# The last norm of an encoder kernel: the last chunk's squares to TensorE in their own parts, a Newton step in two operations, additions split evenly, one program order

## The chip, the core and the metric

The kernel runs on one core of a Trainium2 chip. The metric is the device time of one execution in microseconds (us), lower is better. Three runs of the kernel before took 3162.19, 3160.36 and 3156.84 us; the median is 3160.36 us.

## The reference

One layer over a prompt of 2048 tokens and a sample of 32, 2080 columns in all, with 1024 channels. Attention and gated linear attention come first, then the channel sub-layer. Only the last lines of the layer matter here: a gated MLP gives `yf`, and its RMSNorm, gated per channel, is added to the residual.

```
def rmsnorm(x, g):
    xf = x.astype(jnp.float32)
    r = lax.rsqrt(jnp.mean(xf * xf, axis=-1, keepdims=True) + EPS)
    return (xf * r).astype(x.dtype) * g
...
    yf, conv_new = conv_ffn(h, s_conv, p['w_up'], p['w_dw'], p['b_dw'], p['w_down'])
    x = x + gate_f * rmsnorm(yf, p['g_post_ffn'])
```

## The kernel before, in words

Channels lie on the 128 partitions, tokens along the free dimension; the 1024 output channels are 8 chunks of 128. The tokens are worked in three passes (`p` = 0, 1, 2), and each pass holds two segments of up to 348 columns (`s` = 0, 1), the upper and the lower half of a `[128, 2, 348]` tile. Products are done in a Strassen-like scheme, each in float32r as three matmuls per 128 rows (a high part and a low part of each operand). `prod` (L1869) issues one such product; its matmuls are all recorded at L1882.

The program runs through `UNITS`: first the up projections of the three passes, then nine units of the down projection, each with four blocks `m`. One `block` (L1975) makes four quarter results at once: chunk `m` in `ad` (segment 0 in `ad[:, 0]`, segment 1 in `ad[:, 1]`) and chunk `m + 4` in `g`. In the down projection three units (groups 0 to 2) add up in `ACC[p, c]`, which lies in SBUF. `down_sum` (L1947) does that: VectorE adds the PSUM result to `ACC` (L1955), and in the last group ScalarE squares the sum into `sq` (L1970), VectorE adds the square to the running sum `sa` (L1972), and ScalarE multiplies `ACC` by the gate (L1968, in place). `sa` is thus a sum over chunks, still spread over 128 partitions.

The order is written out by hand. `put(n, f)` appends a step to a list, and `run_due()`, called in every `side()`, takes the steps that are due: with n = 0 at once, with n over 0 at the (n+1)th call. From L1224 on, a `manual_schedule` named `ordered` fixes this order as the program order of TensorE, ScalarE, VectorE, GpSimd and SyncE. It is closed at L2268, ahead of the last steps; from there on only TensorE keeps program order (L82), and the scheduler of the framework orders the instructions of the other engines. `in_order[0] = False` (L2269) makes every `put` immediate.

The last steps belong to the last block of the last unit (pass 2, `last` in the code). It makes chunk 3 in `ad` and chunk 7 in `g`. In order of time: segment 1 of chunk 7 is ready after product S3 (L2013), segment 0 of chunk 3 after product A12, segment 1 of chunk 3 after S4 and the addition L2019, segment 0 of chunk 7 after A22 (L2035). Then `finish(2)` (L2145) does the last norm:

- for each segment, segment 1 first: `split` (L67) makes a high part of `sa` on ScalarE (L69) and a low part on VectorE (L72); two matmuls with a matrix of ones sum both over the partitions into PSUM (L2154, L2155);
- for each segment: Ln and Exp on ScalarE give a first value `r0` of 1/sqrt (L2158, L2159), and three operations on VectorE make a Newton step of it in PSUM (L2160 to L2162);
- for each segment and each of the 8 chunks in `ORDER` = 0, 4, 1, 5, 2, 6, 3, 7: VectorE multiplies `ACC` by the result, from PSUM (L2166), the residual `xs` is added, both operands in SBUF (L2168; positions 2 and 5 on VectorE, the other six on GpSimd), and `move` (L2050) stores the segment with DMAs from the queues of SyncE and ScalarE (L2057). The two stores at the very end, of chunks 3 and 7 in segment 0, are on ScalarE's queue.

The residuals `xs` are loaded some 40 us before the end, and the activation table that holds Ln and Exp is preloaded at the same place (L2249, L2250).

Of the kernel before, what the change touches and what calls it, by code (L numbers as in the profile page):

```python
# [13 lines left out]
AF = mybir.ActivationFunctionType  # L14
OP = mybir.AluOpType
# [4 lines left out]
D = 1024  # L20
KD = 8
TP, TS = 2048, 32
# [5 lines left out]
EPS = 1e-6  # L28
# [15 lines left out]
def f32(ap):  # L44
    return ap.bitcast(F32)
# [13 lines left out]
def encoder_step(ctx: ExitStack, tc: tile.TileContext, I, O):  # L59
    nc = tc.nc  # L60
# [6 lines left out]
    def split(hi, lo, src, keep=False):  # L67

        i = nc.scalar.activation(hi, src, AF.Copy)  # L69
        if keep and not in_order[0]:  # L70
            tc.keep_in_program_order(i)
        nc.vector.tensor_sub(lo, src, f32(hi))  # L72
# [19 lines left out]
    ones = consts.tile([128, 128], F32R, name="ones")  # L92
# [150 lines left out]
    with ExitStack() as st:  # L243
# [115 lines left out]
        r0 = fin0()  # L359
# [1509 lines left out]
    def prod(out, u, m, x, y, first):  # L1869

        while (u, m, x) not in WO or (u, y) not in HO:
            if (u, m, x) not in WO:
                next(wq)
            else:
                hstep()
            run_due()
        wh, wl = WO[u, m, x]
        hi, lo = HO[u, y]
        w, n = WIDTH[u], NK[u]
        for k in range(n):  # L1880
            for i, (l_, r_) in enumerate(((wh, hi), (wh, lo), (wl, hi))):
                nc.tensor.matmul(out[:, :w], l_[:, k], r_[:, k, :w], start=first and k == 0 and i == 0,  # L1882
                                 stop=k == n - 1 and i == 2, skip_group_check=True)
        del LIVE[u, m, x]
        if m == NM[u] - 1:
            del HLIVE[(7 * u + OPS.index(y)) % len(HP)]
# [16 lines left out]
    def act_sums():  # L1903

        if made:
            p, j, x, y = made.pop(0)
            o = WP[p] - 2
            x0, x1, y0, y1 = x[:, 0, :o], x[:, 1, :o], y[:, 0, :o], y[:, 1, :o]

            for i, (out, a, b) in enumerate(((x0, x1, x0), (x1, y1, x1), (y1, y1, x0), (y0, y0, y1))):  # L1910
                put(i, lambda out=out, a=a, b=b: nc.vector.tensor_sub(out, a, b))
            for i, v in ((0, x), (2, y)):
                put(3 + i, lambda i=i, v=v: nc.sync.dma_start(
                    dap(aT, ((4 * p + i) * 11 + j) * 128 * SEG, [[SEG, 128], [11 * 128 * SEG, 2], [1, o]]), v[:, :, :o]))
# [11 lines left out]
    def up_g(p, m, x, y, before):  # L1926

        o, c, d = WP[p] - 2, m + MF, 1

        def act():  # L1930
            nc.vector.tensor_mul(y[:, :, :o], y[:, :, :o], YG[:, :, :o])
            soon(2, lambda: nc.sync.dma_start(actD[p, m, :, :, :o], y[:, :, :o]))
            if m % 2:
                made.append((p, m // 2, before, y))

        if p == 2:
            put(1, lambda: conv_outputs(x[:, 1], c))
        put(d + 1, lambda: tap(2, YG, x, c, o))
        put(d + 2, lambda: tap(1, YG, x, c, o))
        put(d + 3, lambda: tap(0, YG, x, c, o))  # L1940
        put(d + 4, act)
# [5 lines left out]
    def down_sum(p, grp, c, x, first, seg=None, n=0):  # L1947

        o = WP[p] - 2
        if grp == 0:  # L1950
            ACC[p, c] = spare.pop(0)
            put(n, lambda: nc.scalar.copy(ACC[p, c][:, :, :o], x[:, :, :o]))
            return
        a, x, q, t = [v[:, :, :o] if seg is None else v[:, seg, :o] for v in (ACC[p, c], x, sa if first else sq, sa)]
        put(n, lambda: nc.vector.tensor_add(a, a, x))  # L1955
        if grp == 2:
            flat = ACC[p, c].rearrange("p s w -> p (s w)")
            e = SEG + TP - segs[5][0]
            if p < 2:
                parts = [(0, a)]  # L1960
            elif seg is None:
                parts = [(0, flat[:, :e]), (1, flat[:, e:])]
            else:
                parts = [[(0, flat[:, :SEG])], [(0, flat[:, SEG:e]), (1, flat[:, e:])]][seg]

            def gate():
                for s, v in parts:
                    nc.scalar.activation(v, v, AF.Copy, scale=mod[:, 5, c, s:s + 1])  # L1968

            put(n + 1, lambda: nc.scalar.activation(q, a, AF.Square))  # L1970
            if not first:
                put(n + 2, lambda: nc.vector.tensor_add(t, t, q))  # L1972
            put(n + 2, gate)

    def block(u, m, prev, side):  # L1975

        p, grp = UNITS[u]
        at_step[0] = 0  # L1980
        w = WIDTH[u]
        last = u == len(UNITS) - 1 and m == NM[u] - 1
        ad = psA.tile([128, 2, 512], F32, name="ad", tag="ad")
        g = psG.tile([128, 2, 512], F32, name="g", tag="g")
        prod(ad[:, 0], u, m, "A11", "B11", True)
        norm = wanted.pop(0)(ad, g) if wanted else None
        if u == 0 and m < 2:

            nc.tensor.matmul(g[:, 0], WO[u, m, "A11"][0][:, 0], WO[u, m, "A11"][0].rearrange("p k n -> p (k n)"),
                             start=True, stop=True, skip_group_check=True)  # L1990
        nc.scalar.copy(g[:, 0, :w], ad[:, 0, :w])  # L1991
        if norm:
            norm()
        if prev:
            prev[0]()
        side()
        if prev:
            prev[1]()
        side()
        if not prev:  # L2000

            prod(ad[:, 1], u, m, "S1", "T1", True)
        prod(g[:, 0], u, m, "S2", "T2", False)
        nc.scalar.copy(U2[:, :w], g[:, 0, :w])  # L2004
        side()
        if prev:
            prod(ad[:, 1], u, m, "S1", "T1", True)
        nc.scalar.copy(P5[:, :w], ad[:, 1, :w])  # L2008
        side()
        prod(g[:, 0], u, m, "S3", "T3", False)  # L2010
        nc.vector.tensor_add(g[:, 1, :w], g[:, 0, :w], P5[:, :w])
        if last:
            down_sum(p, grp, m + 4, g, False, 1)  # L2013
        side()
        prod(ad[:, 0], u, m, "A12", "B21", False)
        act_sums()
        side()
        prod(ad[:, 1], u, m, "S4", "B22", False)
        nc.vector.tensor_add(ad[:, 1, :w], ad[:, 1, :w], U2[:, :w])  # L2019
        side()  # L2020
        if grp is None:
            YA.append(YA.pop(0))
            before, ya = YA[-2:]

        def rest_ad():
            if grp is None:
                up_ad(p, m, ad, ya)
            elif last:
                for seg in (1, 0):
                    down_sum(p, grp, m, ad, False, seg)  # L2030
            else:
                down_sum(p, grp, m, ad, m == 0, None, 0)

        def rest_g():
            prod(g[:, 0], u, m, "A22", "T4", False)  # L2035
            if grp is None:
                up_g(p, m, g, ya, before)
            else:
                down_sum(p, grp, m + 4, g, False, 0 if last else None, 1)

        return rest_ad, rest_g

# [26 lines left out]
    def post(p):  # L2069
# [55 lines left out]
        for i, m in enumerate(ORDER):  # L2125
# [16 lines left out]

            put(2, store)

    def finish(p):  # L2145

        o = WP[p] - 2
        sh, sl = [x[:, 0:2, :o] for x in HP[(7 * len(UNITS)) % len(HP)]]
        r0 = sq[:, :, :o]
        rs = {}  # L2150
        for s, ps, tag in ((1, psA, "ad"), (0, psG, "g")):
            split(sh[:, s], sl[:, s], sa[:, s, :o])
            rs[s] = q = ps.tile([128, 2, 512], F32, name=tag, tag=tag)[:, s, :o]
            nc.tensor.matmul(q, ones, sh[:, s], start=True, stop=False)  # L2154
            nc.tensor.matmul(q, ones, sl[:, s], start=False, stop=True)  # L2155
        for s in (1, 0):
            q = rs[s]
            nc.scalar.activation(r0[:, s], q, AF.Ln, bias=eps, scale=1.0 / D)  # L2158
            nc.scalar.activation(r0[:, s], r0[:, s], AF.Exp, scale=-0.5)  # L2159
            nc.vector.scalar_tensor_tensor(q, q, D * EPS, r0[:, s], op0=OP.add, op1=OP.mult)  # L2160
            nc.vector.scalar_tensor_tensor(q, q, -0.5 / D, r0[:, s], op0=OP.mult, op1=OP.mult)  # L2161
            nc.vector.scalar_tensor_tensor(q, q, 1.5, r0[:, s], op0=OP.add, op1=OP.mult)  # L2162
            for i, m in enumerate(ORDER):
                acc = ACC[p, m]
                a = acc[:, s, :o]
                nc.vector.tensor_mul(a, a, q)  # L2166
                add = nc.vector if i % 3 == 2 else nc.gpsimd
                add.tensor_add(a, a, xs[m][:, s, :o])  # L2168
                move(p, acc, O["yT"], m, False, s)

    def pend():
        while pending and next(pending[0], 1) == 1:
# [92 lines left out]
            pending.append(post(p))  # L2265
    while due:
        run_due()
    ordered.close()  # L2268
    in_order[0] = False  # L2269
    prev[0]()  # L2270
    prev[1]()
    finish(2)


def _shape_constants():
# [61 lines left out]
```

## Time and profile before

| what | value |
|---|---|
| median of three runs | 3160.36 us (3156.84 to 3162.19) |
| time of the profiled execution | 3162.02 us |
| its span, first to last instruction | 3160.3 us |
| mean granted TensorE clock | 0.991 |
| TensorE matmul busy | 3047.7 us |
| VectorE busy | 2239.8 us |
| ScalarE busy | 1648.8 us |
| GpSimd busy | 269.4 us |

TensorE is busy nearly throughout; VectorE, ScalarE and the DMA queues work beside it. Busy time over the whole span therefore tells little about the last steps, where TensorE has nothing left to multiply. These are read in the timeline: each row gives the start in us from the beginning of the span, the duration in us, the engine, the line, the operation with its tiles (out<-in), its shape and, in square brackets, how long the engine had been idle and what released it. "x2" joins two neighbouring instructions in one row, whose duration then runs from the first start to the last end. The residual's tiles appear as `ht`, `acc` or `hA`, the accumulators as `acc` or `work`.

### The profile page before, as it was taken

Reading aid. Unit: us, or ns where it says so; the run is one execution under the profiler, and the core shown is the slowest. Engines: PE = TensorE matmul, PEld = TensorE weight load, DVE = VectorE, ACT = ScalarE, POOL = GpSimd, SP = SyncE. Lnnn points to the kernel's source line nnn. Section 1 sums busy time; section 2 is a strip of 40 time slices with the busy share of each in tenths; the row PEclk is TensorE's granted clock in tenths of the full one; section 3 lists DMA queues with packets and bytes.
Section 4 is the critical chain, followed back from the end, with each engine's and each line's share of the span. In section 5 each row is a group of like instructions: output and inputs, shape, how many; then the busy total and the mean of one; then the engine's idle time right before and its main releaser. Section 6 shows DMA issues by size and latency. Waiting matters only on the chain. (4 is left out here: it accounts for less than half of the span.)

```text
span 3160.3 us, 56426 instructions
## 1 busy us (share of the span) xinstructions
PE 3047.7 (96%) x19748; PEld 2947.7 (93%) x19748; DVE 2239.8 (71%) x4879; ACT 1648.8 (52%) x3792; POOL 269.4 (9%) x427
## 2 busy tenths in 40 slices
PE   6999999999999999999999999999999999999997
PEld 4899999998999999988999899999999999999997
DVE  6735617774555555566677799998888778897877
ACT  4522224443555555544454655567666556576755
POOL 2201201112111111120000000000000000000001
PEclk9999999999999999999999999999999999999998
DMA  7354435554433334575457686788897667888784
GB/s 220 91 156 125 139 98 142 137 137 128 130 109 111 107 100 117 169 230 184 140 175 227 211 256 210 223 256 225 249 265 217 189 189 230 263 250 284 242 267 146
DMA packets 598478, 580.12 MB, mean 184 GB/s; under 512 B 53201, under 2 KB 526530, under 8 KB 598194
## 3 DMA queue, kind: packets, MB, share of 16 engines
q1 hardware_dynamic: 553026, 527.86, 56.2%
q10 hardware_dynamic: 44432, 47.34, 4.7%
q8 instruction: 155, 2.54, 0.3%
q0 software_dynamic: 736, 1.33, 0.2%
q14 instruction: 129, 1.06, 0.1%
HBM read 388.71 MB, written 187.65 MB: 182 GB/s over the span
## 5 line engine op out<-in xcount | busy, mean ns | idle before, releaser
L1882 PE MATMUL ad<-hA,hB 128*128 128x350 f32 (+2 forms) x1734 | 301.7, 324 | 3.8 <-DVE hB L1824 2.4
L1882 PEld LDWEIGHTS ad<-hA,hB 128*128 128x128 f32 x1734 | 282.5, 189 | 5.5 <-DVE hB L1824 3.3
L78 PE MATMUL pm<-hA,wh 128*128 128x416 f32 x768 | 287.4, 374 | 0.0
L79 PE MATMUL pm<-hA,wh 128*128 128x416 f32 x768 | 269.3, 351 | 0.0
L80 PE MATMUL pm<-hA,wl 128*128 128x416 f32 x768 | 269.3, 351 | 0.0
L1824 DVE TENSOR_TENSOR hA<-raws,hA 128x512 fp32r<-128x512 f32 (+1 forms) x367 | 241.9, 668 | 13.0 <-ACT hA L1819 12.7
L1819 ACT ACTIVATE hA<-raws 128x512 fp32r<-128x512 f32 (+1 forms) x367 | 222.0, 617 | 29.9 <-DMA raws<-in_w_up_dram 11.1
L1882 PE MATMUL ad<-hA,hA 128*128 128x348 f32 (+2 forms) x1308 | 225.5, 323 | 2.5 <-ACT work L2008 1.8
L1882 PE MATMUL g<-hA,hB 128*128 128x348 f32 (+2 forms) x1248 | 217.1, 323 | 6.4 <-ACT work L2004 3.5
L1882 PEld LDWEIGHTS ad<-hA,hA 128*128 128x128 f32 x1308 | 211.8, 188 | 3.9 <-ACT work L2008 2.4
L1882 PEld LDWEIGHTS g<-hA,hB 128*128 128x128 f32 x1248 | 202.3, 188 | 9.1 <-ACT work L2004 4.7
L1882 PE MATMUL ad<-hA 128*128 128x350 f32 (+2 forms) x1173 | 205.1, 324 | 4.2 <-DVE hA L1734 4.1
L1882 PEld LDWEIGHTS ad<-hA 128*128 128x128 f32 x1173 | 191.7, 190 | 5.0 <-DVE hA L1734 4.4
L1824 DVE TENSOR_TENSOR hB<-raws,hB 128x512 fp32r<-128x512 f32 (+1 forms) x289 | 190.9, 668 | 6.5 <-ACT hB L1819 6.1
L1819 ACT ACTIVATE hB<-raws 128x512 fp32r<-128x512 f32 (+1 forms) x289 | 175.8, 617 | 25.3 <-DMA raws<-in_w_up_dram 11.8
L69 ACT ACTIVATE pth<-pp 128x256 fp32r<-128x256 f32 (+1 forms) x288 | 106.4, 373 | 139.2 <-PE pp L1027 135.9
L72 DVE TENSOR_TENSOR ptl<-pp,pth 128x256 fp32r<-128x256 f32 (+1 forms) x288 | 118.1, 414 | 85.2 <-ACT pth L69 82.4
L78 PE MATMUL pn<-wh,hA 128*128 128x256 f32 (+1 forms) x624 | 176.9, 283 | 0.0
L79 PE MATMUL pn<-wl,hA 128*128 128x256 f32 (+1 forms) x624 | 176.3, 283 | 0.0
L80 PE MATMUL pn<-wh,hA 128*128 128x256 f32 (+1 forms) x624 | 176.1, 282 | 0.0
L1991 ACT COPY g<-ad 128x348 f32<-128x348 f32 (+2 forms) x102 | 44.3, 434 | 244.1 <-PE ad L1882 156.4
L1882 PE MATMUL g<-hA,hA 128*128 128x350 f32 (+2 forms) x894 | 157.4, 325 | 4.0 <-ACT g L1991 2.3
(507 smaller groups left out, 8468.6 us busy)
## 6 DMA issues: line engine op xcount, KB each, us to landing
raws<-in_w_up_dram SPq DMA_DIRECT2D x220, 256.0 KB, 4.3
raws<-sW SPq DMA_DIRECT2D x176, 256.0 KB, 3.8
sW<-raws SPq DMA_DIRECT2D x88, 256.0 KB, 3.6
raws<-in_w_down_dram SPq DMA_DIRECT2D x80, 256.0 KB, 5.2
wr<-in_w_in_dram SPq DMA_DIRECT2D x76, 256.0 KB, 3.2
sgT<-tx ACTq DMA_DIRECT2D x80, 208.0 KB, 1.9
wa<-in_w_ada_dram SPq DMA_DIRECT2D x64, 256.0 KB, 3.0
keys<-ks SPq DMA_DIRECT2D x128, 128.0 KB, 2.9
```

The source lines that it names most:

```text
L69: i = nc.scalar.activation(hi, src, AF.Copy)
L72: nc.vector.tensor_sub(lo, src, f32(hi))
L78: nc.tensor.matmul(out, ah, bh, start=first and i == 0, stop=False)
L79: nc.tensor.matmul(out, ah, bl, start=False, stop=False)
L80: nc.tensor.matmul(out, al, bh, start=False, stop=last and i == n - 1)
L1819: act = nc.scalar.activation(hi[:, :n], raw(i, n), AF.Copy)
L1824: nc.vector.tensor_sub(lo[:, :n], raw(i, n), f32(hi[:, :n]))
L1882: nc.tensor.matmul(out[:, :w], l_[:, k], r_[:, k, :w], start=first and k == 0 and i == 0, stop=k == n - 1 and i == 2, skip_group_check=True)
L1991: nc.scalar.copy(g[:, 0, :w], ad[:, 0, :w])
```

## The change

It has five parts, all in the last block and in `finish`.

1. Segment 0 of chunk 3 goes to `down_sum` as soon as product A12 is issued (n = 1), instead of after the last products.
2. The last result of each segment (chunk 3 in segment 1, chunk 7 in segment 0) no longer enters `sa`. A new function `final_add` splits the `sa` so far into a high and a low part, adds the result to `ACC`, and makes the square in two parts: the high part by ScalarE's Square into float32r, the exact square by VectorE (`a * a`), and the low part as their difference. The gate follows. `finish` then sums four parts for each segment on TensorE (four matmuls with ones instead of two).
3. The Newton step: ScalarE squares `r0` (one more activation for each segment), VectorE then needs two operations instead of three, and the factor -0.5/D moves into the multiplication by the norm, which becomes a scalar_tensor_tensor.
4. The additions of the residual alternate: even positions on GpSimd, odd ones on VectorE, so four and four for each segment instead of six and two.
5. `ordered.close()` moves behind `finish(2)`: all of it runs in program order. In that order VectorE does Newton of segment 1, four chunks of segment 1, Newton of segment 0, the other four chunks of segment 1, and the eight of segment 0.

```diff
         prod(ad[:, 0], u, m, "A12", "B21", False)
+        if last:
+            down_sum(p, grp, m, ad, False, 0, 1)
         act_sums()
...
             elif last:
-                for seg in (1, 0):
-                    down_sum(p, grp, m, ad, False, seg)
+                final_add(p, m, 1, ad)
             else:
                 down_sum(p, grp, m, ad, m == 0, None, 0)
...
             prod(g[:, 0], u, m, "A22", "T4", False)
             if grp is None:
                 up_g(p, m, g, ya, before)
+            elif last:
+                final_add(p, m + 4, 0, g)
             else:
-                down_sum(p, grp, m + 4, g, False, 0 if last else None, 1)
+                down_sum(p, grp, m + 4, g, False, None, 1)
...
+    SUMS = {}
+
+    def final_add(p, c, s, x):
+
+        o = WP[p] - 2
+        hi, lo = HP[(7 * len(UNITS)) % len(HP)]
+        a, t = ACC[p, c][:, s, :o], sa[:, s, :o]
+        (sh, qh), (sl, ql) = [[v[:, r + s, :o] for r in (0, 2)] for v in (hi, lo)]
+        split(sh, sl, t)
+        nc.vector.tensor_add(a, a, x[:, s, :o])
+        nc.scalar.activation(qh, a, AF.Square)
+        nc.vector.tensor_mul(t, a, a)
+        nc.vector.tensor_sub(ql, t, f32(qh))
+        flat = ACC[p, c].rearrange("p s w -> p (s w)")
+        e = SEG + TP - segs[5][0]
+        for v, (l, r) in enumerate([(0, SEG)] if s == 0 else [(SEG, e), (e, 2 * SEG)]):
+            nc.scalar.activation(flat[:, l:r], flat[:, l:r], AF.Copy, scale=mod[:, 5, c, v:v + 1])
+        SUMS[s] = (sh, sl, qh, ql)
+
     def finish(p):
 
         o = WP[p] - 2
-        sh, sl = [x[:, 0:2, :o] for x in HP[(7 * len(UNITS)) % len(HP)]]
-        r0 = sq[:, :, :o]
+        r0, t = sq[:, :, :o], sa[:, :, :o]
         rs = {}
         for s, ps, tag in ((1, psA, "ad"), (0, psG, "g")):
-            split(sh[:, s], sl[:, s], sa[:, s, :o])
             rs[s] = q = ps.tile([128, 2, 512], F32, name=tag, tag=tag)[:, s, :o]
-            nc.tensor.matmul(q, ones, sh[:, s], start=True, stop=False)
-            nc.tensor.matmul(q, ones, sl[:, s], start=False, stop=True)
-        for s in (1, 0):
-            q = rs[s]
+            for i, x in enumerate(SUMS[s]):
+                nc.tensor.matmul(q, ones, x, start=i == 0, stop=i == 3)
             nc.scalar.activation(r0[:, s], q, AF.Ln, bias=eps, scale=1.0 / D)
             nc.scalar.activation(r0[:, s], r0[:, s], AF.Exp, scale=-0.5)
-            nc.vector.scalar_tensor_tensor(q, q, D * EPS, r0[:, s], op0=OP.add, op1=OP.mult)
-            nc.vector.scalar_tensor_tensor(q, q, -0.5 / D, r0[:, s], op0=OP.mult, op1=OP.mult)
-            nc.vector.scalar_tensor_tensor(q, q, 1.5, r0[:, s], op0=OP.add, op1=OP.mult)
-            for i, m in enumerate(ORDER):
-                acc = ACC[p, m]
-                a = acc[:, s, :o]
-                nc.vector.tensor_mul(a, a, q)
-                add = nc.vector if i % 3 == 2 else nc.gpsimd
-                add.tensor_add(a, a, xs[m][:, s, :o])
-                move(p, acc, O["yT"], m, False, s)
+            nc.scalar.activation(t[:, s], r0[:, s], AF.Square)
+
+        def newton(s):
+            q = rs[s]
+            nc.vector.scalar_tensor_tensor(q, q, D * EPS, t[:, s], op0=OP.add, op1=OP.mult)
+            nc.vector.scalar_tensor_tensor(q, q, -3.0 * D, r0[:, s], op0=OP.add, op1=OP.mult)
+
+        def scaled(s, i):
+            acc = ACC[p, ORDER[i]]
+            a = acc[:, s, :o]
+            nc.vector.scalar_tensor_tensor(a, a, -0.5 / D, rs[s], op0=OP.mult, op1=OP.mult)
+            add = nc.vector if i % 2 else nc.gpsimd
+            add.tensor_add(a, a, xs[ORDER[i]][:, s, :o])
+            move(p, acc, O["yT"], ORDER[i], False, s)
+
+        newton(1)
+        for i in range(4):
+            scaled(1, i)
+        newton(0)
+        for i in range(4, KD):
+            scaled(1, i)
+        for i in range(KD):
+            scaled(0, i)
...
     while due:
         run_due()
-    ordered.close()
     in_order[0] = False
     prev[0]()
     prev[1]()
     finish(2)
+    ordered.close()
```

## The prediction

> **What bounds the kernel now.** I first read the chain of work that ended last, then the timeline of the last 25 us row by row, then the groups of instructions there, shapes kept apart.
>
> ```profile
> 3149.13 0.45 DVE g L2161
> ...
> 3150.17 0.53 DVE acc L2166
> ...
> 3151.64 1.78 POOL work L2168 x2
> ...
> 3155.75 0.87 POOLq L2326
> ```
>
> Columns: start, us, engine, tile, line. The chain that ended last runs through VectorE's work of the first segment into the Newton step of the second, then through GpSimd's additions to the end. How these steps begin:
>
> ```profile
> 3134.82 1.59 PE L1882 MATMUL g<-hA,hB 128*128 128x348 f32 x9
> ...
> 3135.46 0.51 DVE L1972 TENSOR_TENSOR saF<-saF,sqF 128x348 f32<-128x348 f32 x1
> 3135.89 0.94 DVE L1955 TENSOR_TENSOR acc<-acc,ad 128x348 f32<-128x348 f32 x2
> 3136.43 0.49 ACT L1970 ACTIVATE sqF<-acc 128x348 f32<-128x348 f32 x1 [1.02 <-DVE acc L1955]
> ...
> 3136.95 0.77 ACT L1968 ACTIVATE acc<-acc,mod 128x314 f32<-128x314 f32 x2
> ```
>
> ```profile
> 3138.01 0.48 ACT L69 ACTIVATE hA<-saF 128x348 fp32r<-128x348 f32 x1
> ...
> 3138.40 0.57 ACT L1968 ACTIVATE acc<-acc,mod 128x348 f32<-128x348 f32 x1
> ...
> 3138.58 0.51 DVE L72 TENSOR_TENSOR hA<-saF,hA 128x348 fp32r<-128x348 f32 x1
> 3138.87 0.48 ACT L1970 ACTIVATE sqF<-acc 128x348 f32<-128x348 f32 x1
> ...
> 3139.84 0.55 ACT L2158 ACTIVATE sqF<-ad,eps 128x348 f32<-128x348 f32 x1 [0.49 <-PE ad L2155]
> ...
> 3141.85 0.66 PE L2155 MATMUL g<-hA,ones 128*128 128x348 f32 x1
> 3142.27 0.53 DVE L2161 SCALAR_TENSOR_TENSOR ad<-ad,sqF 128x348 f32<-128x348 f32 x1
> 3142.55 0.55 ACT L2158 ACTIVATE sqF<-g,eps 128x348 f32<-128x348 f32 x1 [0.92 <-PE g L2155]
> 3142.83 0.53 DVE L2162 SCALAR_TENSOR_TENSOR ad<-ad,sqF 128x348 f32<-128x348 f32 x1
> 3143.13 0.49 ACT L2159 ACTIVATE sqF<-sqF 128x348 f32<-128x348 f32 x1
> 3143.66 0.53 DVE L2160 SCALAR_TENSOR_TENSOR g<-g,sqF 128x348 f32<-128x348 f32 x1 [0.30 <-ACT sqF L2159]
> 3144.09 0.51 DVE L2166 TENSOR_TENSOR acc<-acc,ad 128x348 f32<-128x348 f32 x1
> ```
>
> The last product ends at 3134.82 + 1.59 = 3136.41. What the change touches lies almost wholly behind that, and the span ends at 3160.3:
>
> ```profile
> core 0: 3160.3 us, clock 0.991
> ```
>
> So 23.9 us, 0.76% of the span, are in play. I call a change of 0.2% (6.3 us) about the least that a measurement of this kernel can tell from none; a gain of that size needs a quarter of these 23.9 us. They fall into a head (to 3144.09, the first multiplication by the norm), a body (multiplications and additions) and the last stores. The body:
>
> ```profile
> 3144.52 1.36 DVE L2166 TENSOR_TENSOR work<-work,ad 128x348 f32<-128x348 f32 x3
> 3144.83 0.80 POOL L2168 TENSOR_TENSOR acc<-acc,ht 128x348 f32<-128x348 f32 x1 [38.41 <-DVE acc L2166]
> 3145.59 1.84 POOL L2168 TENSOR_TENSOR work<-work,ht 128x348 f32<-128x348 f32 x2
> ...
> 3145.80 0.97 DVE L2168 TENSOR_TENSOR work<-work,ht 128x348 f32<-128x348 f32 x1
> ...
> 3146.69 0.93 DVE L2166 TENSOR_TENSOR work<-work,ad 128x348 f32<-128x348 f32 x2
> ...
> 3147.97 0.74 DVE L2168 TENSOR_TENSOR work<-work,acc 128x348 f32<-128x348 f32 x1
> ...
> 3148.63 0.50 DVE L2166 TENSOR_TENSOR acc<-acc,ad 128x348 f32<-128x348 f32 x1
> ```
>
> ```profile
> 3151.89 1.05 DVE L2168 TENSOR_TENSOR work<-work,ht 128x348 f32<-128x348 f32 x1
> ...
> 3152.86 0.93 DVE L2166 TENSOR_TENSOR work<-work,g 128x348 f32<-128x348 f32 x2
> ...
> 3154.14 0.83 DVE L2168 TENSOR_TENSOR work<-work,acc 128x348 f32<-128x348 f32 x1
> ...
> 3154.90 0.50 DVE L2166 TENSOR_TENSOR acc<-acc,g 128x348 f32<-128x348 f32 x1
> 3155.71 0.91 POOL L2168 TENSOR_TENSOR acc<-acc,hA 128x348 f32<-128x348 f32 x1
> 3155.78 1.21 ACTq L2057 DMA_DIRECT2D out_yT_dram<-acc  x2
> ```
>
> The body lasts from 3144.09 to 3155.71 + 0.91 = 3156.62, that is 12.53 us; the rest, 3.68 us, is the last store's issue, its landing and the end.
>
> **Spacings.** VectorE starts an independent multiplication 0.43 us after the one before (3144.09 to 3144.52), also behind a scalar_tensor_tensor (3143.66 to 3144.09). A step that needs the result of the one right before it comes 0.56 us after (3142.27 to 3142.83). An addition with both operands in SBUF beside GpSimd takes 0.97, 0.74, 1.05 and 0.83 us, and the next step starts after 0.89, 0.66, 0.97 and 0.76. Alone, the same kind takes 0.517:
>
> ```profile
> L1972 DVE TENSOR_TENSOR saF<-saF,sqF 128x348 f32<-128x348 f32 x4 | 2.1, 517 | 0.7 <-ACT sqF L1970 0.7
> ...
> L2166 DVE TENSOR_TENSOR work<-work,ad 128x348 f32<-128x348 f32 x5 | 2.3, 508 | 0.0
> ```
>
> The multiplications, with one operand in PSUM, stay at 0.508 beside the same GpSimd work. So what is slowed is the addition in SBUF, the very thing of which VectorE gets more.
>
> **The head after the change.** I set the new program order out on the old clock. The addition of chunk 3, segment 0, is queued behind L1972 and so starts at 3135.89, where the old row has its first addition. Its Square runs from 3136.43, its gate from 3136.95 (spacing 0.52, as the old rows have it), and now the high part of segment 1's sum stands behind that gate: 0.47 after its start (3138.40 to 3138.87), 3137.42 to 3137.90. VectorE's low part waits for it, 0.09 more (as from 3138.49 to 3138.58): 3137.99. The program puts the addition of chunk 3, segment 1, behind this low part: 3138.42 to 3138.93, where the old kernel had it first, at 3135.89. Square and exact square follow side by side to 3139.47, the low square runs from 3139.50 to 3140.02. ScalarE gates both pieces, 0.77 from 3139.50, and turns to segment 0 before it may take segment 1's Ln: high part 3140.20 to 3140.68, low part on VectorE from 3140.77, addition of chunk 7 from 3141.20 to 3141.71, Square and exact square to 3142.26 (the in-place gate waits for the latter), gate at 3142.29, Ln 0.47 later at 3142.76. In the old kernel Ln stood at 3139.84. From there the change is quick: Exp 0.58 later (3142.55 to 3143.13), its end 3143.83, the new Square to 3144.35, first Newton operation at 3144.42, the second at 3144.97, the first multiplication at 3145.52. That is 2.76 us from Ln, where before it took 4.25 (one Newton operation more; L2160 of segment 0 with its wait of 0.30; an Exp held up by a gate and a high part). Against 3144.09 the head is **1.4 us longer**. TensorE's four matmuls cost nothing of it: the low square's ends by 3140.02 + 0.05 + 0.66 = 3140.73, two us ahead of Ln; if ScalarE were free that is when Ln would start and the head would be 3140.73 + 2.76 - 3144.09 = -0.6. That is the low end; the high end is +2.6, with 0.1 us more at each of a dozen hand-overs.
>
> Segment 0's Newton inputs come from ScalarE by 3144.35 + 3 x 0.55 = 3146.0, needed only after four chunks: hidden. Its Square costs no table load: Square, Ln and Exp all run in this stretch of the timeline, which shows no load between them.
>
> **The body after the change.** A pair of chunks on VectorE: a multiplication whose addition goes to GpSimd (0.43), a multiplication (0.56, its addition needs it), an addition. GpSimd has one addition for each pair, 0.80 to 0.92, starting 0.2 us after the first multiplication: it runs beside nearly all of VectorE's addition, but no second one follows at once as before. So I take the shorter spacings, 0.66 and 0.76, mean 0.71: 1.70 a pair, 13.6 for 8 pairs. Newton of segment 0 lies between, 0.56 + 0.43 = 0.99, and the last addition ends 0.07 after its spacing: 14.66 us, against 12.53, **+2.1 us**. VectorE becomes the bound in GpSimd's place. Bounds: without any contention an addition has the spacing 0.43, a pair 1.42, the body 12.4 (-0.1); with 0.97 each, a pair 1.96 and the body 16.7 (+4.2).
>
> Here the Trainium skill bears on it, "GPSIMD Engine Reference", section "Key points": GpSimd shares its SBUF interfaces with VectorE, and contention comes with VectorE instructions that have two SBUF inputs. By that rule the even split is paid for twice, and the trace agrees (0.74 to 1.05 against 0.517); read without it, the split would come out at -0.1 instead of +2.1. Against the 0.43 stands "VectorE: DVE Perf Modes", section "The DRAIN you can't avoid": the next operation does not start until the pipe is empty, dependent or not. By it each pair would be about 0.1 longer and the body 0.7; the rows show 0.43 beside 0.56, and I go by them.
>
> **The last stores.** Chunk 3's addition (GpSimd) and chunk 7's (VectorE) now end nearly together, and ScalarE issues both stores behind one another; the old row shows two in 1.21, of which one issue is about 0.35. I add **0.25 us** (0 to 0.4).
>
> Sum: 1.4 + 2.1 + 0.25 = +3.8 us. On the profiled execution, 3162.02 us with 1.7 us around its span of 3160.3, that is 3165.8; it lies 1.7 above the median, so on 3160.36 the forecast is **3164.1 us**, 0.12% more.
>
> **Rivals.** *The cheap split.* VectorE's additions fall into the gaps of GpSimd's, the body is 12.4, and ScalarE is free for segment 1 earlier (head -0.6): -0.1 - 0.6 + 0.25 gives -0.5 us, 3159.9 us. For it: GpSimd is busy only about half of the time. Against it: in the written order both additions of a pair start within 0.4 us of each other, and ScalarE's order is fixed. Chance 0.17.
>
> *Contention throughout.* Each of the eight additions on VectorE pays as the first of each old segment did, spacing 0.97, because GpSimd's addition always starts just ahead of it: body +4.2. With the head and the stores, +5.9; with multiplications beside it spaced by their full 0.51, 8 x 0.08 more: +6.5, 3166.9 us, slower by over 0.2%. It decides from additions of about 1.0 us on. For it: 0.97 and 1.05 among four rows. Against it: those two had a second GpSimd addition behind the first. Chance 0.13.
>
> The forecast keeps 0.70.
>
> **How the numbers follow.** 3159.9 and 3166.9 are the outer cases. The three old runs lie from 1.8 us above to 3.5 below their median, so a median of such runs may be an us off: 3158.8 to 3168.0 holds 8 in 10. Slower by over 0.2% (above 3166.7): most of the last rival and little else, 0.10. Faster by over 0.2% needs -6.3 us, more than any case gives, 0.03. Within it 0.87.
>
> **What would show it.** Right: Ln of segment 1 about 6.4 us after the last product's end, behind the gate of chunk 7; the first scalar_tensor_tensor of the body 9.1 us after it; VectorE gapless in the body, GpSimd with gaps; VectorE's additions between 0.7 and 0.85. Wrong: Ln before segment 0's high part, additions near 0.52 (first rival) or near 1.0 with a body of 16 us or more (second), or any difference ahead of 3131 us, where the two programs are to be alike.

## The result and the profile after

Over 22 runs each, the changed kernel took 3166.1 us in the median (3161.43 to 3171.81) and the kernel before 3160.81 (3156.33 to 3164.97). The ratio is 1.0018 with a 95% interval of 1.0012 to 1.0024: 0.18% slower, 5.3 us, where 3.8 us more had been forecast. The profiled execution's span:

```profile
core 0: 3169.7 us, clock 0.989
```

That is 9.4 us more than the old profile's, but only part of it comes from the change: this execution was the slowest of the 22. The head of the last norm in the changed kernel's timeline (start, us, engine, line, operation):

```profile
3139.39 1.59 PE L1882 MATMUL g<-hA,hB 128*128 128x348 f32 x9
...
3140.46 0.51 DVE L1955 TENSOR_TENSOR acc<-acc,ad 128x348 f32<-128x348 f32 x1
...
3142.02 0.48 ACT L69 ACTIVATE hA<-saF 128x348 fp32r<-128x348 f32 x1
3142.53 0.52 DVE L72 TENSOR_TENSOR hA<-saF,hA 128x348 fp32r<-128x348 f32 x1 [0.48 <-ACT hA L69]
...
3142.97 0.51 DVE L2157 TENSOR_TENSOR acc<-acc,ad 128x348 f32<-128x348 f32 x1
...
3146.29 0.49 ACT L2158 ACTIVATE hA<-acc 128x348 fp32r<-128x348 f32 x1 [1.01 <-DVE acc L2157]
...
3146.91 0.58 ACT L2164 ACTIVATE acc<-acc,mod 128x348 f32<-128x348 f32 x1
...
3147.40 0.53 ACT L2176 ACTIVATE sqF<-ad,eps 128x348 f32<-128x348 f32 x1
...
3148.49 0.49 ACT L2178 ACTIVATE saF<-sqF 128x348 f32<-128x348 f32 x1
...
3149.01 0.53 DVE L2182 SCALAR_TENSOR_TENSOR ad<-ad,saF 128x348 f32<-128x348 f32 x1 [1.58 <-ACT saF L2178]
...
3149.58 0.53 DVE L2183 SCALAR_TENSOR_TENSOR ad<-ad,sqF 128x348 f32<-128x348 f32 x1
...
3150.14 0.52 DVE L2188 SCALAR_TENSOR_TENSOR acc<-acc,ad 128x348 f32<-128x348 f32 x1
```

The last product ends at 3140.98, 4.57 us later than in the old profile (3136.41). TensorE's program is the same up to there, in the runs below this end lies anywhere from 3134.1 to 3140.2, and the timed executions of the changed kernel alone are up to 10.4 us apart (3161.43 to 3171.81); so I take it for scatter of single executions. So the kernels are compared by the stretch from the end of the last product to the end of the span: 23.9 us before, 3169.7 - 3140.98 = 28.7 us now, **4.8 us more**, 0.15% and inside the interval of the timed runs.

In the head, the addition of chunk 3 (L2157) stands on VectorE behind the low part L72, which waits for the high part L69, and Ln (L2176) stands behind the Square and the gate of segment 0's last chunk (L2158, L2164). Ln begins 6.42 us after the last product (before: 3.43), the first multiplication 9.16 after it (before: 7.68).

The body, from the same timeline, the first pair and two later ones, then the end:

```profile
3150.57 0.51 DVE L2188 SCALAR_TENSOR_TENSOR work<-work,ad 128x348 f32<-128x348 f32 x1
3150.88 0.80 POOL L2190 TENSOR_TENSOR acc<-acc,ht 128x348 f32<-128x348 f32 x1 [39.88 <-DVE acc L2188]
3151.17 0.89 DVE L2190 TENSOR_TENSOR work<-work,ht 128x348 f32<-128x348 f32 x1
...
3159.26 0.92 POOL L2190 TENSOR_TENSOR acc<-acc,ht 128x348 f32<-128x348 f32 x1 [0.88 <-DVE acc L2188]
3159.64 0.91 DVE L2190 TENSOR_TENSOR work<-work,ht 128x348 f32<-128x348 f32 x1
3160.47 0.93 DVE L2188 SCALAR_TENSOR_TENSOR work<-work,g 128x348 f32<-128x348 f32 x2
...
3161.05 0.92 POOL L2190 TENSOR_TENSOR work<-work,ht 128x348 f32<-128x348 f32 x1 [0.88 <-DVE work L2188]
3161.44 0.91 DVE L2190 TENSOR_TENSOR work<-work,ht 128x348 f32<-128x348 f32 x1
...
3165.04 0.91 DVE L2190 TENSOR_TENSOR acc<-acc,hA 128x348 f32<-128x348 f32 x1
3165.61 0.82 ACTq L2060 DMA_DIRECT2D out_yT_dram<-acc  x2
```

A pair lasts 1.80 us (3159.64 to 3161.44). GpSimd is idle 0.88 us or more between its additions, VectorE never; the bound has moved from GpSimd to VectorE. The body lasts from 3150.14 to 3165.95, 15.81 us against 12.53. The chain that ended last, which before ran through GpSimd's additions, is VectorE alone in its last pieces:

```profile
3160.55 0.87 DVE work L2188 x2
...
3161.44 0.91 DVE work L2190
```

And these rows say more. GpSimd's addition ends at 3150.88 + 0.80 = 3151.68, VectorE's at 3152.06, 0.38 later; at 3160.18 and 3160.55, 0.37 later; at 3161.97 and 3162.35, 0.38 later. All eight VectorE additions end 0.37 to 0.38 us after GpSimd's, however long before that they began. The old profile has the same. Four of GpSimd's additions there, as single rows, each the one that runs when one of the four VectorE additions that the prediction quotes begins:

```profile
3145.59 0.80 POOL L2168 TENSOR_TENSOR work<-work,ht 128x348 f32<-128x348 f32 x1
...
3147.41 0.92 POOL L2168 TENSOR_TENSOR work<-work,acc 128x348 f32<-128x348 f32 x1
...
3151.64 0.91 POOL L2168 TENSOR_TENSOR work<-work,ht 128x348 f32<-128x348 f32 x1
...
3153.68 0.91 POOL L2168 TENSOR_TENSOR work<-work,acc 128x348 f32<-128x348 f32 x1
```

They end at 3146.39, 3148.33, 3152.55 and 3154.59, VectorE's at 3146.77, 3148.71, 3152.94 and 3154.97, each 0.38 or 0.39 later.

### The profile page after: what moved, and what is told of

Same layout as the page of the kernel before. It is cut to its first block, busy times and chain, and to the rows that moved or that the text cites. A ratio compares the mean times of both kernels' runs of the same rounds, so it can differ in the third digit from the quotient of the medians.

```text
span 3169.7 us, 56439 instructions
## 1 busy us (share of the span) xinstructions
PE 3054.4 (96%) x19752; PEld 2953.6 (93%) x19752; DVE 2244.5 (71%) x4883; ACT 1652.0 (52%) x3794; POOL 264.0 (8%) x423
## 5 line engine op out<-in xcount | busy, mean ns | idle before, releaser
L1819 ACT ACTIVATE hB<-raws 128x512 fp32r<-128x512 f32 (+1 forms) x289 | 175.8, 617 | 24.0 <-DMA raws<-in_w_up_dram 10.4
L69 ACT ACTIVATE pth<-pp 128x256 fp32r<-128x256 f32 (+1 forms) x288 | 106.7, 374 | 139.0 <-PE pp L1027 134.2
L72 DVE TENSOR_TENSOR ptl<-pp,pth 128x256 fp32r<-128x256 f32 (+1 forms) x288 | 118.2, 414 | 85.2 <-ACT pth L69 82.6
```

The source lines that it names most:

```text
L1819: act = nc.scalar.activation(hi[:, :n], raw(i, n), AF.Copy)
```

## The experiments

The theory, after the result: VectorE's addition with both operands in SBUF does not share with a running GpSimd addition; it is *held* until that ends, and then needs its 0.37. And the head is long because of the queue on ScalarE. The rival for the body is a picture closer to the prediction's, which let VectorE's addition run beside GpSimd's: both going on at about half rate; the rival for the head is that the two-part square makes the chain itself longer.

One table for all runs, in us. Ln and the first multiplication (mult) count from the end of the last product; the body runs from there to the end of the last addition, the store from that to the end of the span. Each is worked out from the profile's timeline as above; the span is printed to 0.1, so the store and the stretch are good to 0.05. The body, the head and the store come from one profiled execution of each kernel.

| kernel | Ln | mult | body | store | stretch | ratio to before (95%) |
|---|---|---|---|---|---|---|
| before | 3.43 | 7.68 | 12.53 | 3.68 | 23.9 | 1 |
| changed | 6.42 | 9.16 | 15.81 | 3.75 | 28.7 | 1.0018 (1.0012 to 1.0024) |
| e1_split_6_2 | 6.42 | 9.16 | 13.48 | 3.75 | 26.4 | 1.0009 (1.0000 to 1.0019) |
| e2_long_gpsimd | 6.42 | 9.16 | 18.76 | 3.66 | 31.6 | not timed |
| e3_ln_first | 4.20 | 7.25 | 15.82 | 3.69 | 26.8 | 1.0008 (0.9998 to 1.0017) |
| e4_skewed | 6.41 | 9.15 | 11.77 | 3.76 | 24.7 | 1.0001 (0.9991 to 1.0011) |
| e5_rewritten | 2.26 | 5.02 | 13.07 | 4.79 | 22.9 | 1.0002 (0.9993 to 1.0011) |
| e6_even_split_alone | 3.20 | 7.45 | 11.87 | 4.00 | 23.3 | not timed |
| e7_free_order | 3.09 | 6.18 | 11.87 | 3.78 | 21.8 | 0.9983 (0.9974 to 0.9992) |
| e8_written_order_alone | 5.83 | 8.63 | 16.02 | 3.69 | 28.3 | not timed |
| e9_no_early_read | 2.68 | 5.44 | 13.07 | 3.71 | 22.2 | 0.9994 (0.9985 to 1.0003) |

### The old split in the changed kernel (e1_split_6_2)

```diff
-            add = nc.vector if i % 2 else nc.gpsimd
+            add = nc.vector if i % 3 == 2 else nc.gpsimd
```

> The changed kernel with the old split of the additions (positions 2 and 5 of each segment on VectorE, six on GpSimd); all else as changed. In the changed kernel the stretch from the end of the last product to the end of the span is 28.7 us: 9.2 to the first scalar_tensor_tensor of the body, 15.8 of body, 3.7 of last store. Theory (held addition): a VectorE addition with both operands in SBUF makes no step while a GpSimd addition runs and ends 0.37 us after it; so each of the eight holds VectorE, and four of them fewer leave GpSimd as the bound again: body 12.5 to 13.2, stretch 25.4 to 26.1, the whole about 2.9 us less than the changed kernel, that is 0.04% to 0.09% above the kernel before. Rival (the written order and the dependent pairs, not the split, make the body long): four additions fewer save VectorE only their own 0.56 us each, body 13.6 or more.

The stretch was 26.4, 2.3 us less than in the changed kernel; the body, 13.48, lies between the two expectations and nearer the rival's bound, so this run does not decide. Its rows show why the sum was off:

```profile
3147.32 0.80 POOL L2190 TENSOR_TENSOR acc<-acc,ht 128x348 f32<-128x348 f32 x1 [39.89 <-DVE acc L2188]
3148.04 0.52 DVE L2190 TENSOR_TENSOR work<-work,ht 128x348 f32<-128x348 f32 x1
...
3150.62 0.92 POOL L2190 TENSOR_TENSOR work<-work,acc 128x348 f32<-128x348 f32 x1 [0.62 <-DMA out_yT_dram<-work]
...
3150.92 1.00 DVE L2190 TENSOR_TENSOR work<-work,acc 128x348 f32<-128x348 f32 x1
```

The first VectorE addition began as GpSimd's was ending (3148.12) and took 0.52; the second began 0.30 after a GpSimd addition had begun and took 1.00. And GpSimd ran dry for 0.62 us where VectorE's order has the Newton step of segment 0, and for 1.02 behind the held addition, neither of which I had counted. (The rows name a DMA as what ended these waits, which is the profile's inference; the multiplications that GpSimd needs stand behind those steps on VectorE.) What can be kept is the measured part: with the old split, 2.3 of the body's loss of 3.3 us are gone.

### Longer additions on GpSimd (e2_long_gpsimd)

```diff
+            if s == 0 and i % 2 == 0:
+                out = raws_[:, 512 * i:512 * i + 2 * SEG].rearrange("p (s w) -> p s w", w=SEG)
+                nc.gpsimd.tensor_add(out[:, :, :o], acc[:, :, :o], xs[ORDER[i]][:, :, :o])
+                move(p, out, O["yT"], ORDER[i], False, s)
+                return
```

> The changed kernel, but in segment 0 each of GpSimd's four additions works on both segments at once (696 columns instead of 348, into a scratch tile, from which segment 0 is stored); segment 1 is the control. Theory (held addition): GpSimd's addition takes 1.55 to 1.75 us, VectorE's own of 348 columns still ends 0.37 after it and so lasts 1.6 to 1.8 instead of 0.91; a pair in segment 0 takes 2.5 to 2.7 instead of 1.80, the body about 19 us. Rival (shared at about half the rate while both run, as the prediction had it): VectorE's addition needs no more than it has now, 0.9 to 1.0, a pair 1.8, the body 16 to 16.5, whatever the length of GpSimd's.

```profile
3153.35 1.53 POOL L2191 TENSOR_TENSOR raws<-acc,ht 128x696 f32<-128x696 f32 x1 [0.94 <-DVE acc L2188]
3153.68 1.58 DVE L2195 TENSOR_TENSOR work<-work,ht 128x348 f32<-128x348 f32 x1
...
3158.32 1.65 POOL L2191 TENSOR_TENSOR raws<-work,acc 128x696 f32<-128x696 f32 x1 [0.95 <-DVE work L2188]
3158.64 1.72 DVE L2195 TENSOR_TENSOR work<-work,acc 128x348 f32<-128x348 f32 x1
```

VectorE's addition, unchanged in itself, took 1.58 to 1.72 us in segment 0, and in the two rows shown it again ended 0.38 and 0.39 after GpSimd's (3154.88 to 3155.26, 3159.97 to 3160.36). The body was 18.76, as the theory had it (about 19; rival 16 to 16.5). Sharing at half rate is out: the addition is held.

### Each VectorE addition one multiplication later (e4_skewed)

```diff
+            if i % 2:
+                held.append((s, i))
+                return
+            added(nc.gpsimd, s, i)
+            while held:
+                added(nc.vector, *held.pop())
```

> The changed kernel with each of VectorE's additions put one multiplication later in the program: multiplication of the odd chunk, multiplication of the next even chunk, then the odd chunk's addition. Theory (held addition): the addition now starts when GpSimd's is nearly over, its end stays 0.37 behind the end of GpSimd's, VectorE loses less waiting: a pair 1.2 to 1.4 instead of 1.80, body 11.9 to 12.9 instead of 15.8, the whole 2.9 to 3.9 us less than the changed kernel. Rival (shared at half rate): only the 0.13 of the dependent start is saved, a pair 1.65 or more, body 14.5 or more.

```profile
3150.81 0.52 DVE L2190 TENSOR_TENSOR work<-work,ht 128x348 f32<-128x348 f32 x1
...
3150.97 1.13 POOL L2190 TENSOR_TENSOR work<-work,ht 128x348 f32<-128x348 f32 x1 [0.15 <-DVE work L2196]
3151.24 0.94 DVE L2196 SCALAR_TENSOR_TENSOR work<-work,g 128x348 f32<-128x348 f32 x2
...
3152.09 0.51 DVE L2190 TENSOR_TENSOR work<-work,ht 128x348 f32<-128x348 f32 x1
```

A pair now takes 1.28 us (3150.81 to 3152.09), three VectorE instructions at 0.43. Six of VectorE's eight additions take their bare 0.51; only the first and the last, 0.63 and 0.69, still wait for GpSimd's and end 0.38 after it, as the theory had all of them. In segment 0 it is GpSimd's addition that begins while VectorE's is running, and it is the longer for it, 1.13 instead of 0.92 (it ends at 3152.10, 0.77 after VectorE's end at 3151.33): the holding goes both ways, the one that began first goes on, and here it falls on the engine that has time. The body went from 15.81 to 11.77, below the old kernel's, with the same instructions. Stretch 24.7.

### Ln of segment 1 ahead of segment 0's last chunk (e3_ln_first)

```diff
         split(sh, sl, t)
         nc.vector.tensor_add(a, a, x[:, s, :o])
-        nc.scalar.activation(qh, a, AF.Square)
...
+        if s:
+            rest()
+        else:
+            late.append(rest)
...
+            if s == 0:
+                late.pop()()
```

`rest` holds the Square, the low square and the gates; for segment 0 the Newton step of segment 1 goes ahead of the low square.

> The changed kernel with ScalarE's Square and gate of the last chunk in segment 0, and VectorE's low square of it, put behind Ln, Exp and Square and the Newton step of segment 1; nothing is left out. Theory (the head is long because Ln of segment 1 is queued on ScalarE behind segment 0's work): Ln starts 4.3 us after the last product's end instead of 6.4, the first multiplication of the body at 7.5 instead of 9.2, body as it was, the whole 1.6 us less than the changed kernel. Rival (the head is long because the chain through the square's two parts and four matmuls is longer): Ln stays at 6 us or more and nothing is gained.

```profile
3138.84 0.54 ACT L2196 ACTIVATE sqF<-ad,eps 128x348 f32<-128x348 f32 x1
...
3140.34 0.48 ACT L2162 ACTIVATE hA<-acc 128x348 fp32r<-128x348 f32 x1
...
3141.89 0.51 DVE L2203 SCALAR_TENSOR_TENSOR acc<-acc,ad 128x348 f32<-128x348 f32 x1
```

Ln is now ahead of that Square, 4.20 us after the last product (3134.64), the first multiplication at 7.25, and the body is unchanged at 15.82: 1.9 us of the head were segment 0's steps ahead of Ln in ScalarE's queue. What is left, 7.25, is already less than the old kernel's 7.68.

### The change without its program order (e7_free_order)

```diff
     while due:
         run_due()
+    ordered.close()
     in_order[0] = False
...
-    ordered.close()
```

> The changed kernel with part 5 undone: the manual order closed where it was closed before, so the scheduler orders the last steps of ScalarE, VectorE, GpSimd and SyncE; the scheduler's order has chunk 3's addition ahead of the low part, the gate of chunk 7 behind Ln and Exp, and nearly every addition on VectorE one multiplication later. Theory (the written order makes the loss): Ln about 3.1 us after the last product's end, first multiplication at 6.2, body 11.8 to 12.4, stretch 21.6 to 22.4, which is about 2 us less than the kernel before and 6 to 7 less than the changed one. Rival (parts 1 to 4 are slower by themselves): stretch above 23.9.

```profile
3138.86 0.55 ACT L2176 ACTIVATE sqF<-ad,eps 128x348 f32<-128x348 f32 x1
...
3139.84 0.57 ACT L2164 ACTIVATE acc<-acc,mod 128x348 f32<-128x348 f32 x1
...
3141.95 0.52 DVE L2188 SCALAR_TENSOR_TENSOR acc<-acc,ad 128x348 f32<-128x348 f32 x1
...
3149.58 0.51 DVE L2190 TENSOR_TENSOR work<-work,ht 128x348 f32<-128x348 f32 x1
3149.74 1.14 POOL L2190 TENSOR_TENSOR work<-work,ht 128x348 f32<-128x348 f32 x1
```

With the last product's end at 3135.77, Ln (3.09), first multiplication (6.18), body (11.87) and stretch (21.8) all came as the theory had them. The gate now stands behind Ln, and five of the eight additions on VectorE take 0.51 (the others 0.63, 0.73 and 0.70). This kernel is faster than both others: 0.9983 of the kernel before (0.9974 to 0.9992). Of that 0.17% the stretch explains 2.1 us, 0.07%, which lies just outside the interval (0.08% to 0.26%). Where the rest comes from stays open: the profiles show no place for it, and the median of the kernel before itself differed between the sets of runs, 3160.8 to 3164.1. Parts 1 to 4 are a gain; part 5 makes of them a loss.

### The even split alone, and the program order alone, in the kernel before

```diff
-                add = nc.vector if i % 3 == 2 else nc.gpsimd
+                add = nc.vector if i % 2 else nc.gpsimd
```

> The kernel before with the even split alone (additions of odd positions on VectorE), the order left to the scheduler, which puts most of VectorE's additions one multiplication behind their own. Theory (an addition on VectorE costs much only where GpSimd's has long to run beside it): VectorE is the bound, 16 multiplications and 8 additions at 0.43 and two Newton operations at 0.56, with some waiting, body 11.6 to 12.4 instead of 12.5, stretch 23.0 to 23.8. Rival (the even split costs by itself, whatever the order): body 13.5 or more, stretch 25 or more.

```profile
3151.66 0.61 DVE L2168 TENSOR_TENSOR work<-work,ht 128x348 f32<-128x348 f32 x1
...
3153.04 0.51 DVE L2168 TENSOR_TENSOR work<-work,ht 128x348 f32<-128x348 f32 x1
```

With the scheduler's order, which also puts VectorE's additions later, the even split cut the body from 12.53 to 11.87, and the stretch is 23.3, as the theory had both. The split does not cost by itself; it costs where the addition stands right behind its own multiplication, and so right behind the start of GpSimd's.

The other is the kernel before with nothing but the program order changed:

```diff
     while due:
         run_due()
-    ordered.close()
     in_order[0] = False
...
     finish(2)
+    ordered.close()
```

> The kernel before with part 5 alone: its last steps in the order in which they were written. There Ln of segment 0 stands on ScalarE behind all of segment 1's stores, whose issue waits for the additions. Theory (order decides): Ln of segment 1 at about 5.2 us after the last product's end (before: 3.4), first multiplication at 8.0 (7.7), and a gap in VectorE's work of 2 to 4 us between the segments; stretch 27 to 28.5 against 23.9. Rival (the order costs little by itself): stretch below 25.5.

```profile
3151.12 0.55 ACT L2158 ACTIVATE sqF<-g,eps 128x348 f32<-128x348 f32 x1 [8.46 <-DMA out_yT_dram<-work]
...
3152.23 0.53 DVE L2160 SCALAR_TENSOR_TENSOR g<-g,sqF 128x348 f32<-128x348 f32 x1 [3.12 <-ACT sqF L2159]
```

Ln of segment 0 stands behind segment 1's stores in ScalarE's queue, VectorE waits 3.12 us between the segments, and the stretch is 28.3 instead of 23.9, inside the theory's range; Ln of segment 1 (5.83) and the first multiplication (8.63) came 0.6 us later than it had them. Fixing the order of the old steps costs 4.4 us, nearly as much as the whole change did (4.8).

### A program order written anew (e5_rewritten, e9_no_early_read)

The core of the order, on ScalarE and VectorE together:

```diff
+        nc.scalar.activation(qh[1], a31, AF.Square)
+        nc.scalar.activation(sh[1], t[:, 1], AF.Copy)
+        nc.vector.tensor_mul(r0[:, 1], a31, a31)
+        nc.vector.tensor_sub(ql[1], r0[:, 1], f32(qh[1]))
+        nc.vector.tensor_sub(sl[1], t[:, 1], f32(sh[1]))
+        root(1)
...
+        newton(1)
+        scaled(1, 0)
+        scaled(1, 1)
+        nc.vector.tensor_sub(ql[0], r0[:, 0], f32(qh[0]))
+        nc.vector.tensor_sub(sl[0], t[:, 0], f32(sh[0]))
+        root(0)
```

> All parts of the change kept, the last steps written in another program order: chunk 3's two additions to the accumulator stand right behind the instructions that finish its results, nothing of segment 0 stands ahead of Ln, Exp and Square of segment 1 on ScalarE, all gates of chunks 3 and 7 behind those, segment 0's two low parts behind the first two multiplications of the body, and each of VectorE's additions one multiplication later. Theory (the loss comes from two places of the written order, the queue ahead of Ln and the additions held beside GpSimd's): Ln about 2.1 us after the last product's end, the first multiplication at 4.9 instead of 9.2, body 12.4 to 13 including the two low parts (0.86), stretch 21.0 to 21.8 against 23.9 in the kernel before and 28.7 in the changed one: 0.05% to 0.1% faster than before. Rival (two-part square and Newton step are themselves slower): stretch 24 or more.

The head came nearly as expected (2.26 and 5.02), and the body, 13.07, just above its range; the stretch did not: 22.9, because the last store took 4.79 instead of about 3.7. And it hides a further loss ahead of the last product:

```profile
3136.02 0.51 DVE L2018 TENSOR_TENSOR acc<-acc,ad 128x348 f32<-128x348 f32 x1
...
3136.58 1.42 PEld L1882 LDWEIGHTS ad<-hA 128*128 128x128 f32 x9 [1.31 <-DVE acc L2018]
3136.58 1.72 PE L1882 MATMUL ad<-hA 128*128 128x348 f32 x9 [1.03 <-DVE acc L2018]
```

I had put chunk 3's addition of segment 0 ahead of product S4. VectorE then read `ad` while TensorE was to write the other half of the same tile, and TensorE was made to wait 1.03 us for it. The next run moves this, and with it ScalarE's square of that sum, which now stands behind the Square of segment 1:

```diff
-        if last:
-            o_, a3 = WP[p] - 2, ACC[p, m]
-            nc.vector.tensor_add(a3[:, 0, :o_], a3[:, 0, :o_], ad[:, 0, :o_])
...
+            for s_ in (1, 0):
+                nc.vector.tensor_add(a3[:, s_, :o_], a3[:, s_, :o_], ad[:, s_, :o_])
```

> The rewritten order of the run e5_rewritten, but chunk 3's addition of segment 0 stands behind product S4 and its addition L2019, not ahead of them. In e5_rewritten TensorE waited 1.03 us ahead of product S4, released by that addition, and the span ended 4.8 us after the last addition instead of 3.7. Theory (VectorE's early reading of the PSUM tile keeps TensorE from writing into its other half): the wait is gone, TensorE runs S4 without a gap, Ln comes 0.4 us later (2.7 after the last product's end), body 13.1, stretch 22.2 to 22.5 with a last store of 3.7; taken from the start of product A12, where the two products before the last begin, the end comes 26.7 to 27.0 us later, against 28.6 in e5_rewritten, 28.4 in the kernel before and 26.3 in e7_free_order. Rival (the wait has another cause): the gap stays, 28 us or more from that start. A last store near 4.8 again would belong to this order; one near 3.7 would make it scatter.

The wait is gone, Ln came at 2.68, the stretch was 22.2, the end 26.7 us after the start of product A12, and the last store took 3.71 again, so I take the 4.79 of e5_rewritten, a single execution, for scatter. With 0.9994 (0.9985 to 1.0003) it cannot be told from the kernel before. Its head is 0.7 us shorter than that of e7_free_order, its body 1.2 longer, because segment 0's two low parts stand in it. They take 1.41 us there (3146.49 to 3147.90), not the 0.86 that the expectation of e5_rewritten had, since the first of them has both operands in SBUF too and is held:

```profile
3146.37 0.80 POOL L2184 TENSOR_TENSOR acc<-acc,ht 128x348 f32<-128x348 f32 x1 [36.17 <-DVE acc L2189]
3146.49 1.06 DVE L2216 TENSOR_TENSOR hA<-sqF,hA 128x348 fp32r<-128x348 f32 x1
```

It ends at 3147.55, 0.38 after GpSimd's addition (3147.17). The rule that was found for the additions was not applied to the other instruction of this kind.

## Why the prediction was right, and where its sizes were off

**The head was right, step by step.** Ln was forecast 6.4 us after the last product and came at 6.42; the first multiplication at 9.1, and came at 9.16; 1.4 us longer than before, and it was 1.48. The reason held too: in e3_ln_first segment 0's steps in ScalarE's queue were worth 1.9 us.

**The body was right in its sign and in naming contention as the cause, and too small: +2.1 forecast, +3.28 measured.** The term that failed is the spacing of VectorE's addition. I took the mean of the shorter old spacings, 0.66 and 0.76, because no second GpSimd addition follows at once; measured were 0.80 to 0.92 (3159.64 to 3160.47 is 0.83), and over eight pairs this is the missing 1.1 us.

The reason for the choice was wrong. Nothing is shared between the two: e2_long_gpsimd shows the addition held until GpSimd's ends. The second GpSimd addition had no part in the long spacings of the old profile, 0.89 and 0.97: those VectorE additions ended 0.38 after the first one, at 3146.77 and 3152.94. The short spacings were additions that began later in GpSimd's (0.46 to 0.56 us after its start, against 0.21 to 0.25), not ones that suffered less. The old rows had shown it in their ends, and I had read their durations. With the end of GpSimd's addition the pair follows: it starts 0.15 to 0.30 after the multiplication ahead of VectorE's addition, runs 0.80 to 0.92, and VectorE's next step starts 0.30 after it ends, 0.08 before the held addition is over. In segment 0 that is 0.43 + 0.15 + 0.92 + 0.30 = 1.80.

The rows agree with what the Trainium skill says in "GPSIMD Engine Reference", section "Key points", that VectorE instructions with two SBUF inputs contend with GpSimd. Of the other rule weighed (the Trainium skill, "VectorE: DVE Perf Modes", section "The DRAIN you can't avoid") the prediction gave one half, that the next operation waits for an empty pipe; the same section adds that a next operation that is not held (its word, for another thing than the hold shown here) starts earlier. The rows show the earlier start: an independent multiplication began 0.43 us after the start of one of 0.52 (3150.14 to 3150.57).

**The last stores:** 0.25 us forecast, 0.07 measured.

**The sum** of the measured terms is 1.48 + 3.28 + 0.07 = 4.8 us. The forecast, 3164.1, was 2.0 us under the measured 3166.1, inside its range: 1.0 us of that is this sum, 0.45 the median of the kernel before (3160.81 over 22 runs, 3160.36 over the three it started from), and the rest is within the interval of the timed runs. I had called 0.2% about the least that can be told from none; with 22 runs each the interval was 0.06% either way, and 0.18% is clear of zero.

**The rivals.** The cheap split did not come in the written order, and came in another: e4_skewed and e7_free_order have a body of 11.8 to 11.9, under the 12.4 that I gave it. Contention throughout (spacing 0.97, additions of about 1.0, body 16.7), to which I gave 0.13, was nearer to the measured body, 15.81, than the forecast's 14.66, and nearer in its reason: GpSimd's addition did always start just ahead of VectorE's, by 0.29 to 0.38 us. The additions took 0.88 to 1.00, mean about 0.93.

**The signs named for it** were there except one: Ln came behind chunk 7's gate, VectorE ran without gaps in the body, GpSimd with gaps, but VectorE's additions did not take 0.7 to 0.85. Their 0.88 to 1.00 lies between that and the second rival's sign, as the body does. One sign of being wrong was badly chosen: that the profiles be alike ahead of 3131 us. Single executions differ there by several us with the same program.

## What to carry to other kernels

A trace row beside another engine's row has an end as well as a duration: when several stretched instructions all end the same time after a neighbour's end, they were held. Here issuing them one multiplication later brought the body to 11.77, and having half as many of them to 13.48. Work that is moved to an idle engine is paid for by what the two share; the same even split gained 0.7 us in one order and lost in another. Before a scheduler's order is replaced by a written one, each engine's queue should be read from the last deadline backwards: here a gate and a Square that had time stood ahead of the one instruction that had none.

## What was not expected of the hardware

VectorE's addition with both operands in SBUF and GpSimd's addition held each other off in every run: 0.51 us became 0.88 to 1.00 beside a GpSimd addition of 0.80 to 0.92, and 1.58 to 1.72 beside one of 1.53 to 1.65, the end 0.37 to 0.39 after GpSimd's in each of these; a GpSimd addition that began 0.16 us into VectorE's took 1.13 instead of 0.92. The body's multiplications by a PSUM operand kept 0.50 to 0.52 throughout.
